# Passage from w_out to the up projection: two operand tiles made beside w_out's last blocks, the embedding's product placed behind w_out, banks and pools laid by order of release

## The chip, the cores and the metric

The kernel runs on one core of a Trainium2 chip. A core has a matrix engine (TensorE, PE in the profile, its weight loads PEld), three engines for elementwise work (VectorE DVE, ScalarE ACT, GpSimd POOL) and a queue engine (SyncE, SP) that here only issues transfers. Each engine runs its own instructions strictly in order and waits where an operand or a buffer of another engine isn't ready. On-chip data lie in SBUF (128 partitions); matmuls write PSUM, whose banks (128x512 fp32 in this program) are handed out by pools too. The metric is the device time of one execution in microseconds (us); less is better.

## What is computed

One decoder layer on x (1 x 1024 x 1024). What matters here is the end of the mixing block, the gated MLP and the per-layer embedding:

```python
h = h + jnp.concatenate([o_a, o_b, o_c], axis=-1) @ w_out[l]
h = h + conv_glu_ffn(rmsnorm(h, norm_ffn_g[l]), ffn_up[l], ffn_conv_w[l], ffn_conv_b[l], ffn_down[l])
gate = jax.nn.sigmoid(rmsnorm(h, norm_ple_g[l]) @ ple_gate[l])
h = h + gate * (p[l] @ ple_proj[l])
...
def conv_glu_ffn(hn, w_up, conv_w, conv_b, w_down):
    u = hn @ w_up                       # 1024 x 5632
    uc = causal depthwise conv of width 3 over u, plus conv_b
    gate, val = jnp.split(uc, 2, axis=-1)
    return (jax.nn.silu(gate) * val) @ w_down
```

`p[l] @ ple_proj[l]` (1024x256 by 256x1024) depends on inputs alone, so it can be computed at any place.

## The kernel before

Activations lie transposed: a tile `h[m]` has 128 of the 1024 features on its partitions and the 1024 positions along its free axis, in two halves of 512. An fp32 product is made of three matmuls on a high and a low part: hi by hi (L127), low of x by hi of w (L129), hi of x by low of w (L131). A high part is a cast on ACT (`whi` L104, operand tiles L1112), a low part a subtraction, for weights of `split_w` on POOL or DVE in turn, by the parity of a counter that also numbers names (L106), for operand tiles on DVE (L1113).

**w_out** (`phase_out`, L1054). Eight blocks of 128 output features. The first pass makes half 0 of all eight blocks, and both halves of blocks 0 and 1; the second pass makes half 1 of blocks 2 to 7. One block of one half is 24 matmuls. Behind a block stand its addition to `h` on DVE (L1073), a store of `h` to DRAM (`hd`, L1074), a square on ACT (L188) and a running sum `acc` on DVE (L189). At the end of each pass `rstd_bcast` makes the norm's factor: four small matmuls sum `acc` over partitions (L159, `ps_ss`), DVE scales (L161), POOL raises to the power -1/2 (L167), four matmuls spread the result over the partitions (L169).

**Operands of the up projection** (`ffn_norm` L1115, `ffn_operands` L1126). `ffn_norm` multiplies `h` by factor and gain (L1122), half 0 first, and splits half 0 into the operand tiles p1 (features 0 to 511) and p2 (the others). The up projection is done in a fast scheme of seven half-size products p1 to p7; p6, p5, p7, p3, p4 need sums of parts of `h` of both halves (L1179, L1181, L1189), and their own splits. `ffn_operands` then issues, for the first two of 22 units: weight loads `raw`, `rav`, the split of the p1 weights, the loads and splits of `pT` and `ple_proj` (L1147, L1148, through the tiles `wraw` of the weights), the products p1 into two G banks, a copy `e` of them to SBUF on ACT (`keep_first`, L1201), the products p2 added onto the same banks, and then the embedding's product: eight blocks of 12 matmuls into V banks, each copied out on ACT (L1167) and stored (L1168) to DRAM for later. After that come p6 to p4 and the loop over units (`phase_up`, L1205): six or seven products of 12 matmuls a unit (L1094), sums of weights on DVE, splits, and behind each unit the convolution, SiLU and gate on ACT and DVE (L1286 to L1295), whose results go to DRAM.

**Down projection** (`phase_down`, L1327). Seven runs over 11 steps k: load `xraw` (L1397), load weights `sr` (L1354), cast and low part of x into `dx` (L1399, L1400), split of the weight, 12 matmuls (L1403). At steps 6 to 9 of the first run `h` is reloaded (L1420).

The order within each engine isn't the order of the code: a scheduler at build time places the instructions, subject to data and to buffers. Which buffer a tile reuses, and so which earlier work it waits for, is set by the pools: a pool that opens takes the room of one that closed, and its first tile waits for the last user of that room.

Of the kernel before, what the change touches and what calls it, by code (L numbers as in the profile page):

```python
# [18 lines left out]
P = 128  # L19
T = 1024  # L20
HT = 512
ND = 8
NFF = 22
EPS = 1e-6
# [4 lines left out]
PC_MIX, PC_FFN, PC_PLE, PC_FIN = 0, 8, 16, 24  # L29
# [50 lines left out]
class Trunk:  # L80
# [57 lines left out]
    def xall(self):  # L138

        X = [({}, {}) for _ in range(ND)]  # L140
        for h in (1, 0):
            for k in range(ND):
                X[k][0][h] = self.xpool.tile([P, HT], F32R, tag=f"xh{k}_{h}", name=self.nm("xh"), bufs=1)
                X[k][1][h] = self.xpool.tile([P, HT], F32R, tag=f"xl{k}_{h}", name=self.nm("xl"), bufs=1)
        return X
# [54 lines left out]
    def build(self):  # L200
        tc, nc = self.tc, self.nc
        with ExitStack() as st:
# [5 lines left out]
            mix, psm = ExitStack(), ExitStack()  # L208
            self.xpool = mix.enter_context(self.pool("x"))
# [7 lines left out]
            up, hs = ExitStack(), ExitStack()  # L217
            self.ep = up.enter_context(self.pool("ep", side="right"))
            hp = hs.enter_context(self.pool("h", side="right"))
# [834 lines left out]
    def phase_out(self, hp, op):  # L1054
# [5 lines left out]
        pbs = []  # L1060
        for hf in (0, 1):
            sl = slice(hf * HT, (hf + 1) * HT)
            acc = op.tile([P, HT], F32, tag="acc", name=self.nm("acc"))
            for m in range(ND):
                t = self.h[m][:, sl]
                if m > 1 or hf == 0:
                    w = self.load_w(self.a["w_out"][m])
                    ps = self.dps.tile([P, T], F32, tag="dp", name=self.nm("dp"))
                    halves = (0, 1) if m < 2 else (hf,)
                    self.dense([ps[:, :HT], ps[:, HT:]], w, self.O, (6, 7, 0, 1, 4, 2, 3, 5), halves)  # L1070
                    for g in halves:
                        u = self.h[m][:, g * HT:(g + 1) * HT]
                        nc.vector.tensor_tensor(u, u, ps[:, g * HT:(g + 1) * HT], ALU.add)  # L1073
                        nc.scalar.dma_start(self.hd[m][g], u)  # L1074
                self.sq_acc(acc, t, m == 0)
            pbs.append(self.rstd_bcast(acc, 1.0 / 1024, EPS, self.mxp))
        return pbs
# [37 lines left out]
    def ffn_norm(self, pbs):  # L1115

        self.TX = {}
        self.op_tiles(self.tpool, "p7", "p6", "p1", "p2", "p5")
        for hf in (0, 1):
            for k in (0, 1, 2, 3, 4, 5, 6, 7) if hf == 0 else (0, 4, 1, 5, 2, 6, 3, 7):  # L1120
                t = self.h[k][:, hf * HT:(hf + 1) * HT]
                self.nc.vector.scalar_tensor_tensor(t, t, self.par[:, PC_FFN + k:PC_FFN + k + 1], pbs[hf],  # L1122
                                                    ALU.mult, ALU.mult)
                if hf == 0:
                    self.op_split("p2" if k >= 4 else "p1", k % 4, t)

    def ffn_operands(self, hs, up):


        nc, h = self.nc, self.h  # L1130
        V, G = nc.vector, nc.gpsimd
        split = self.op_split
        self.units = [{"f": f} for f in range(NFF)]
        first = self.units[:2]
        for d in first:
            d["raw"], d["rav"] = self.load_up(d["f"]), self.load_up(NFF + d["f"])
            d["w1"] = self.split2(d["raw"][:, :HT], V)
        with self.pool("pe") as pp:
            pX, pw = [], []
            for k in (0, 1):  # L1140
                for src, dst, n in ((self.a["pT"][k], pX, "px"), (self.a["ple_proj"][k], pw, "pw")):
                    raw = self.wpool.tile([P, T], F32, tag="wraw", name=self.nm("wraw"), bufs=2)
                    nc.sync.dma_start(raw, src)
                    hi = pp.tile([P, T], F32R, name=self.nm(n + "h"))
                    lo = pp.tile([P, T], F32R, name=self.nm(n + "l"))
                    for c in (slice(0, HT), slice(HT, T)):
                        nc.scalar.copy(hi[:, c], raw[:, c])  # L1147
                        V.tensor_tensor(lo[:, c], raw[:, c], hi[:, c].bitcast(F32), ALU.subtract)  # L1148
                    dst.append((hi, lo))
            self.ped = [self.zpool.tile([P, T], F32, tag=f"pe{m}", name=f"pe{m}") for m in range(ND)]  # L1150
            for d in first:
                d["G"] = self.banks("g")
            self.mul(*[(d["G"][:, :HT], d["w1"], self.TX["p1"], True) for d in first])
            for d in first:
                self.keep_first(d)
            for d in first:
                d["w2"] = self.split2(d["raw"][:, HT:], V)
            self.mul(*[(d["G"][:, :HT], d["w2"], self.TX["p2"], False) for d in first])
            for m in range(ND):
                ps = self.banks("v")  # L1160
                s = slice(m * P, (m + 1) * P)
                for k in (0, 1):
                    (wh, wl), (xh, xl) = pw[k], pX[k]
                    self.mm3({0: ps[:, :HT], 1: ps[:, HT:]}, (wh[:, s], wl[:, s]),
                             ({0: xh[:, :HT], 1: xh[:, HT:]}, {0: xl[:, :HT], 1: xl[:, HT:]}), k == 0, k == 1)
                t = self.wpool.tile([P, T], F32, tag="wraw", name=self.nm("pst"), bufs=2)
                nc.scalar.copy(t, ps)  # L1167
                nc.scalar.dma_start(self.ped[m], t)  # L1168
# [34 lines left out]
    def phase_up(self):  # L1203
        nc, par, ep, cv, TX = self.nc, self.par, self.ep, self.cv, self.TX
        V, G = nc.vector, nc.gpsimd  # L1205
# [24 lines left out]
        def unit(d, prev):  # L1230
# [28 lines left out]
            d["V"] = self.banks("v")  # L1259
# [68 lines left out]
    def phase_down(self, ple):  # L1328
# [14 lines left out]
        for k in (0, 1):  # L1343
            S[k] = xr.tile([P, HT], F32, name=f"sr{k}")
# [212 lines left out]
```

## Time and profile before

| what | value |
|---|---|
| three runs | 1571.83, 1572.70, 1573.13 us (median 1572.7) |
| profiled execution | 1572.51 us, of it the span of the trace 1570.7 us, 1.8 us outside |
| mean granted TensorE clock | 0.974 of full speed |
| w_out's last matmul | issued at 771.98 us of the span |
| first matmul of p6 (the up projection's loop) | 824.97 us |
| first matmul of the down projection | 1233.00 us |

A row of the timeline gives the start in us of the span, the duration, engine, line, operation, result and operand, shape, how many like it follow each other, and in brackets how long the engine stood idle before it and for whom it waited. Matmul durations overlap with each other: what one costs is the distance from start to start. The granted clock is what the chip let TensorE run at in a stretch, 1.00 being full speed.

### The profile page before, as it was taken

Reading aid. Unit: us, or ns where it says so; the run is one execution under the profiler, and the core shown is the slowest. Engines: PE = TensorE matmul, PEld = TensorE weight load, DVE = VectorE, ACT = ScalarE, POOL = GpSimd, SP = SyncE. Lnnn points to the kernel's source line nnn. Section 1 sums busy time; section 2 is a strip of 40 time slices with the busy share of each in tenths; the row PEclk is TensorE's granted clock in tenths of the full one; section 3 lists DMA queues with packets and bytes.
Section 4 is the critical chain, followed back from the end, with each engine's and each line's share of the span. In section 5 each row is a group of like instructions: output and inputs, shape, how many; then the busy total and the mean of one; then the engine's idle time right before and its main releaser. Section 6 shows DMA issues by size and latency. Waiting matters only on the chain.

```text
span 1570.7 us, 20134 instructions
## 1 busy us (share of the span) xinstructions
PE 1490.0 (95%) x7480; PEld 1227.9 (78%) x7480; DVE 1099.8 (70%) x1578; ACT 630.2 (40%) x1079; POOL 429.7 (27%) x353
## 2 busy tenths in 40 slices
PE   7989999989999989999879999999999999999996
PEld 5768998778987777777768888888888778888774
DVE  6378453368547568844768888888888779877584
ACT  6331331322424455523445444444444435455441
POOL 2231411132412123113123455544454000002330
PEclk9989999999999999999999999999999999999998
DMA  5212202123024032054323333333331793351352
GB/s 192 71 58 91 74 28 81 41 74 107 28 84 139 28 108 74 28 202 147 121 110 104 101 101 108 108 101 109 106 113 70 241 327 116 101 167 51 110 173 84
DMA packets 78707, 167.84 MB, mean 107 GB/s; under 512 B 19920, under 2 KB 20048, under 8 KB 78608
## 3 DMA queue, kind: packets, MB, share of 16 engines
q1 hardware_dynamic: 65120, 145.97, 28.6%
q10 hardware_dynamic: 12400, 16.52, 3.1%
q0 software_dynamic: 1088, 4.06, 0.8%
q8 instruction: 59, 0.97, 0.3%
q14 instruction: 40, 0.33, 0.1%
HBM read 120.12 MB, written 46.40 MB: 106 GB/s over the span
## 4 chain that ended last, share of the span: by engine, by line
PE 43%; issue 19%; DVE 5%; POOL 1%; ACT 1%; DMA 1%; POOLq 0%; SPq 0%; DVEq 0%; ACTq 0%
PE bg L1094 15%; PE bv L1094 11%; PE hsc L849 2%; PE swq L993 1%; PE dp L129 1%; PE dp L131 1%; PE dp L127 1%; PE bv L131 1%; PE bv L127 1%; PE swo L1029 1%; PE bv L129 1%; PE swt L1016 1%; PE zp L127 1%; PE zp L129 1%; PE zp L131 1%
## 5 line engine op out<-in xcount | busy, mean ns | idle before, releaser
L127 PE MATMUL dp<-xh,whi 128*128 128x512 f32 x544 | 186.9, 401 | 13.7 <-ACT xh L344 8.6
L131 PE MATMUL dp<-xh,wlo 128*128 128x512 f32 x544 | 185.1, 398 | 1.0 <-POOL wlo L106 1.0
L129 PE MATMUL dp<-xl,whi 128*128 128x512 f32 x544 | 185.3, 398 | 0.7 <-DVE xl L345 0.6
L104 ACT CAST whi<-wraw 128x512 fp32r<-128x512 f32 x120 | 73.4, 619 | 234.5 <-PE dp L129 181.6
L106 POOL TENSOR_TENSOR wlo<-wraw,whi 128x512 fp32r<-128x512 f32 x60 | 83.4, 1390 | 283.6 <-ACT whi L104 242.2
L106 POOL TENSOR_TENSOR wlo<-raw,whi 128x512 fp32r<-128x512 f32 x84 | 134.9, 1624 | 92.7 <-ACT whi L104 92.6
L127 PEld LDWEIGHTS dp<-xh,whi 128*128 128x128 f32 x544 | 103.4, 191 | 36.0 <-ACT xh L344 8.6
L129 PEld LDWEIGHTS dp<-xl,whi 128*128 128x128 f32 x544 | 102.9, 190 | 25.0 <-DVE xl L345 3.0
L131 PEld LDWEIGHTS dp<-xh,wlo 128*128 128x128 f32 x544 | 103.3, 191 | 22.4 <-POOL wlo L106 1.9
L106 POOL TENSOR_TENSOR wlo<-s,whi 128x512 fp32r<-128x512 f32 x44 | 68.0, 1545 | 164.0 <-ACT whi L104 164.0
L1403 PE MATMUL bg<-dx,whi 128*128 128x512 f32 x308 | 96.8, 395 | 2.5 <-DVE dx L1400 2.4
L1403 PE MATMUL bv<-dx,whi 128*128 128x512 f32 x308 | 95.5, 391 | 0.0
L104 ACT CAST whi<-raw 128x512 fp32r<-128x512 f32 x88 | 52.4, 619 | 99.6 <-issue 50.9
L104 ACT CAST whi<-s 128x512 fp32r<-128x512 f32 x66 | 39.0, 619 | 114.8 <-PE bg L1094 112.4
L167 POOL TENSOR_TENSOR rst<-rst,mhalf 128x4 f32<-128x4 f32 x8 | 9.3, 1159 | 257.5 <-DVE rst L161 257.4
L106 DVE TENSOR_TENSOR wlo<-wraw,whi 128x512 fp32r<-128x512 f32 x60 | 50.6, 849 | 41.3 <-ACT whi L104 38.1
L1403 PEld LDWEIGHTS bg<-dx,whi 128*128 128x128 f32 x308 | 57.3, 189 | 17.7 <-ACT whi L104 3.5
L1403 PEld LDWEIGHTS bv<-dx,whi 128*128 128x128 f32 x308 | 58.1, 189 | 12.3
L1399 ACT CAST dx<-xraw 128x512 fp32r<-128x512 f32 x77 | 47.9, 622 | 49.1 <-PE bv L1403 28.1
L1400 DVE TENSOR_TENSOR dx<-xraw,dx 128x512 fp32r<-128x512 f32 x77 | 54.8, 712 | 4.8 <-ACT dx L1399 4.6
L286 DVE TENSOR_TENSOR dp<-dp,rstd 128x512 f32<-128x512 f32 (+1 forms) x26 | 23.2, 898 | 46.6 <-PE dp L131 44.7
L1403 PE MATMUL bg<-dx,wlo 128*128 128x512 f32 x154 | 48.0, 393 | 1.1 <-DVE wlo L106 1.1
(403 smaller groups left out, 3871.8 us busy)
## 6 DMA issues: line engine op xcount, KB each, us to landing
raw<-in_ffn_up_dram SPq DMA_DIRECT2D x44, 512.0 KB, 3.7
wraw<-in_w_in_dram SPq DMA_DIRECT2D x30, 512.0 KB, 3.7
z<-zst SPq DMA_DIRECT2D x18, 512.0 KB, 3.2
gb<-ct SPq DMA_DIRECT2D x33, 256.0 KB, 2.3
xraw<-gb SPq DMA_DIRECT2D x33, 256.0 KB, 2.8
xraw<-gt SPq DMA_DIRECT2D x33, 256.0 KB, 2.7
zl<-z SPq DMA_DIRECT2D x16, 512.0 KB, 4.3
wraw<-in_ple_gate_dram SPq DMA_DIRECT2D x16, 512.0 KB, 3.7
```

The source lines that it names most:

```text
L104: nc.scalar.copy(hi, src)
L106: eng.tensor_tensor(lo, src, hi.bitcast(F32), ALU.subtract)
L127: nc.tensor.matmul(ps[hf], wh, xh[hf], start=first, stop=False)
L129: nc.tensor.matmul(ps[hf], wh, xl[hf], start=False, stop=False)
L131: nc.tensor.matmul(ps[hf], wl, xh[hf], start=False, stop=last)
L286: self.nc.vector.tensor_tensor(ps, ps, r, ALU.mult)
L849: nc.tensor.matmul(sc[:, c, :], ks[:, c * P:(c + 1) * P], view(qt, c * P, [2 * n, 64 // n], [HT + n, 2], [1, n]), start=True, stop=True)
L993: nc.tensor.matmul(pq[h][:, b:b + w], d["q"][hs, qb * P:nk], d["k"][hs, b:b + w], start=True, stop=True)
L1094: nc.tensor.matmul(ps, w[part == 2][:, s], X[k][part == 1], start=start and k == part == 0, stop=k == 3 and part == 2, skip_group_check=no ...
L1399: nc.scalar.copy(xh, x)
L1400: V.tensor_tensor(xl, x, xh.bitcast(F32), ALU.subtract)
L1403: nc.tensor.matmul(ps[m], wt[part == 2][:, m * P:(m + 1) * P], (xh, xl)[part == 1], start=k == part == 0, stop=k == NK - 1 and part == 2)
```

## The change

The two passes of w_out and what follows are put together in another way. Half 0 is finished first, then block 2 of half 1, and then the factor of half 0. Blocks 3 to 7 of half 1 follow, and between them, two steps to a block, half 0 is normed and split into p1 and p2; `pT` and `ple_proj` are loaded and split there too, through tiles of their own. The factor of half 1 is made at the end, the first units' weights are loaded and split, and the embedding's product follows w_out directly, into the banks (`dps`) that w_out used. Then come the norm of half 1, p1, the copies `e`, p2, and the other operands.

To make room, the split x tiles lie in one pool for each half; half 0's closes early. p1 and p2 have a pool of their own. The V banks are claimed before the G banks. In the down projection the tiles `xraw`, `dx` and two of the weights `sr` lie on the right side, in the place of others, and the remaining `sr` and the reloaded `h` on the left.

```diff
-                X[k][0][h] = self.xpool.tile([P, HT], F32R, tag=f"xh{k}_{h}", name=self.nm("xh"), bufs=1)
+                X[k][0][h] = self.xpool[h].tile([P, HT], F32R, tag=f"xh{k}", name=self.nm("xh"), bufs=1)
...
-            pbs = self.phase_out(hp, mix.enter_context(self.pool("acc")))
-            mix.close()
+            with self.pool("px", side="right") as self.pxp:
+                pb = self.phase_out(hp, mix[0])
+            mix[1].close()
+            self.ffn_norm(1, pb)
+            psm.close()
             self.tpool = up.enter_context(self.pool("tx"))
-            self.ffn_norm(pbs)
-            psm.close()
+            self.op_tiles(self.tpool, "p6", "p5", "p7")
...
+        for m in range(ND):
+            rows(m, (0, 1) if m < 2 else (0,))
+            self.sq_acc(acc, self.h[m][:, :HT], m == 0)
+        rows(2, (1,))
+        pb = self.rstd_bcast(acc, 1.0 / 1024, EPS, self.mxp)
+        x0.close()
+        self.TX = {}
+        self.op_tiles(self.tp12, "p1", "p2")
+        self.ped = [self.zpool.tile([P, T], F32, tag=f"pe{m}", name=f"pe{m}") for m in range(ND)]
+        with self.pool("pw") as pwp:
+            px, pw = [], []
+            parts = [(px, self.pxp, "pT", 0), (pw, pwp, "ple_proj", 0), (px, self.pxp, "pT", 1), (pw, pwp, "ple_proj", 1)]
+            norm = self.ffn_norm(0, pb)
+            for m in range(3, ND):
+                rows(m, (1,))
+                for _ in range(2):
+                    next(norm, None)
+                if parts:
+                    self.pe_load(pwp, *parts.pop(0))
             for m in range(ND):
...
+                self.sq_acc(acc, self.h[m][:, HT:], m == 0)
+            pb = self.rstd_bcast(acc, 1.0 / 1024, EPS, self.mxp)
+            self.ffn_first()
+            for m in range(ND):
+                ps = self.dps.tile([P, T], F32, tag="dp", name=self.nm("dp"))
+                s = slice(m * P, (m + 1) * P)
+                for k in (0, 1):
+                    (wh, wl), (xh, xl) = pw[k], px[k]
+                    self.mm3({0: ps[:, :HT], 1: ps[:, HT:]}, (wh[:, s], wl[:, s]),
+                             ({0: xh[:, :HT], 1: xh[:, HT:]}, {0: xl[:, :HT], 1: xl[:, HT:]}), k == 0, k == 1)
+                t = self.wpool.tile([P, T], F32, tag="wraw", name=self.nm("pst"), bufs=2)
+                nc.scalar.copy(t, ps)
+                nc.scalar.dma_start(self.ped[m], t)
+        return pb
+
+    def pe_load(self, raws, dst, pool, src, k):
+        raw = raws.tile([P, T], F32, tag="praw", name=self.nm("praw"), bufs=2)
+        self.nc.sync.dma_start(raw, self.a[src][k])
+        hi, lo = (pool.tile([P, T], F32R, name=self.nm(n)) for n in ("peh", "pel"))
+        for c in (slice(0, HT), slice(HT, T)):
+            self.nc.scalar.copy(hi[:, c], raw[:, c])
+            self.nc.vector.tensor_tensor(lo[:, c], raw[:, c], hi[:, c].bitcast(F32), ALU.subtract)
+        dst.append((hi, lo))
...
         for d in first:
...
+            d["V"] = self.banks("v")
+        for d in first:
+            d["G"] = self.banks("g")
+        self.mul(*[(d["G"][:, :HT], d["w1"], self.TX["p1"], True) for d in first])
+        for d in first:
+            self.keep_first(d)
+        for d in first:
+            d["w2"] = self.split2(d["raw"][:, HT:], V)
+        self.mul(*[(d["G"][:, :HT], d["w2"], self.TX["p2"], False) for d in first])
...
-        hp = ple.enter_context(self.pool("h2", side="right"))
+        xr = ple.enter_context(self.pool("xr", side="right"))
+        xb = [xr.tile([P, HT], F32R, name=f"dx{i}") for i in range(8)]
+        xs = [xr.tile([P, HT], F32, name=f"xraw{i}") for i in range(6)]
+        S = {k: xr.tile([P, HT], F32, name=f"sr{k}") for k in (0, 1)}
         wst = self.wst = ple.enter_context(self.pool("ws", side="right"))
         wa = aa.enter_context(self.pool("wa", side="right"))
-        xr = ple.enter_context(self.pool("xr"))
-        S = {}
-        for k in (6, 7, 8, 9, 10, 2, 3, 4, 5):
-            S[k] = xr.tile([P, HT], F32, name=f"sr{k}")
-        xb = [xr.tile([P, HT], F32R, name=f"dx{i}") for i in range(8)]
-        xs = [xr.tile([P, HT], F32, name=f"xraw{i}") for i in range(6)]
-        for k in (0, 1):
-            S[k] = xr.tile([P, HT], F32, name=f"sr{k}")
+        xl = ple.enter_context(self.pool("xl"))
+        for k in range(2, NK):
+            S[k] = xl.tile([P, HT], F32, name=f"sr{k}")
+        hp = ple.enter_context(self.pool("h2"))
```

What the scheduler makes of it stands in the instruction orders. Each row has the line, the operation, and result and operands by their numbered names. The first place is PE at the end of w_out, before: behind the last matmul of w_out (`dp`) stand the sum of squares of half 1, the spread of its factor and the first matmuls of p1.

```order
L127 MATMUL dp_6065<-xh_5367,whi_6061 128x512
L129 MATMUL dp_6065<-xl_5368,whi_6061 128x512
L131 MATMUL dp_6065<-xh_5367,wlo_6063 128x512
L159 MATMUL ps_ss_6095<-few,acc_5850 128x1 x4
L169 MATMUL ps_ss_6096<-cst,rst_1233_6103 128x128 x4
L1094 MATMUL bg_6250<-tp1h_6130,whi_6195 128x512
L1094 MATMUL bg_6251<-tp1h_6130,whi_6203 128x512
```

The same place after the change (`peh` and `pel` are the embedding's operands, `dp` its banks):

```order
L131 MATMUL dp_6135<-xh_5370,wlo_6133 128x512
L127 MATMUL dp_6214<-peh_5966,peh_6017 128x512 x2
L129 MATMUL dp_6214<-pel_5967,peh_6017 128x512 x2
L131 MATMUL dp_6214<-peh_5966,pel_6018 128x512 x2
L127 MATMUL dp_6214<-peh_6068,peh_6119 128x512 x2
L129 MATMUL dp_6214<-pel_6069,peh_6119 128x512 x2
L131 MATMUL dp_6214<-peh_6068,pel_6120 128x512 x2
L127 MATMUL dp_6230<-peh_5966,peh_6017 128x512 x2
L159 MATMUL ps_ss_6184<-few,acc 128x1 x4
L129 MATMUL dp_6230<-pel_5967,peh_6017 128x512 x2
L169 MATMUL ps_ss_6185<-cst,rst_1243_6192 128x128 x4
L131 MATMUL dp_6230<-peh_5966,pel_6018 128x512 x2
```

Between the last matmul of w_out and the sum of squares now stand 14 matmuls of the embedding, and two more ahead of the spread; p1 comes after all 96 of them.

The second place is ACT ahead of the copies `e` of p1, before (`tp5h`, `tp6h` are operand tiles of p5 and p6, `nu` a sum of parts of `h`):

```order
L1112 CAST tp5h_6146<-h_5433 128x512
L1112 CAST tp5h_6148<-h_5434 128x512
L1112 CAST tp6h_6122<-nu_6442 128x512
L1112 CAST tp6h_6124<-nu_6447 128x512
L1112 CAST tp5h_6150<-h_5435 128x512
L1112 CAST tp6h_6126<-nu_6453 128x512
L1112 CAST tp5h_6152<-h_5436 128x512
L104 CAST whi_6618<-s_1282_6605 128x512
L1201 COPY e_6276<-bg_6250 128x512
```

And after (`pst` is the copy of an embedding block on its way to DRAM):

```order
L1109 COPY pst_6339<-dp_6326 128x1024
L1155 CAST tp6h_6358<-nu_6450 128x512
L1110 DMA pe_5917<-pst_6339 128x1024
L1155 CAST tp6h_6360<-nu_6455 128x512
L1155 CAST tp6h_6362<-nu_6461 128x512
L1155 CAST tp5h_6366<-h_5439 128x512
L1155 CAST tp5h_6368<-h_5440 128x512
L1155 CAST tp5h_6370<-h_5441 128x512
L1155 CAST tp6h_6364<-nu_6467 128x512
L1155 CAST tp5h_6372<-h_5442 128x512
L1225 COPY e_6413<-bg_6387 128x512
```

The eight casts still stand ahead of the copies, now behind the last embedding block.

The third place is the passage to the down projection. ACT before (`ct` is the convolution's result, first of unit 20 and then of unit 21, `dx` the cast x and `whi` from `sr` the cast weight of the down projection):

```order
L1290 ACTIVATE ct_9691<-ct_9691 128x1024
L1286 ACTIVATE ct_9724<-bv_9540,par,ncw 128x1024
L1399 CAST dx_9852<-xraw_9860 128x512
L1286 ACTIVATE ct_9791<-bg_9663,par 128x1024
L104 CAST whi_9910<-sr_9866 128x512
L1399 CAST dx_9854<-xraw_9861 128x512
L104 CAST whi_9930<-sr_9867 128x512
```

ACT after:

```order
L1315 ACTIVATE ct_9697<-ct_9697 128x1024
L1311 ACTIVATE ct_9730<-bv_9546,par,ncw 128x1024
L1311 ACTIVATE ct_9797<-bg_9669,par 128x1024
L1311 ACTIVATE ct_9815<-bv_9702,par,ncw 128x1024
L1315 ACTIVATE ct_9797<-ct_9797 128x1024
L1423 CAST dx_9841<-xraw_9849 128x512
L104 CAST whi_9920<-sr_9855 128x512
```

The first cast of x now stands behind all three activations of the last unit. SP's queue there, before (`gb` and `gt` are gated results stored to DRAM):

```order
L1298 DMA gb_6534<-ct_9691 128x512
L1312 DMA gt_6600<-t_1846_9816 128x512
L1397 DMA xraw_9860<-gb_6524 128x512
L1354 DMA sr_9866<-in_ffn_down_dram 128x512
L1397 DMA xraw_9861<-gb_6525 128x512
```

SP after:

```order
L1323 DMA gb_6542<-ct_9697 128x512
L1337 DMA gt_6608<-t_1844_9822 128x512
L1378 DMA sr_9866<-in_ffn_down_dram 128x512
L1378 DMA sr_9867<-in_ffn_down_dram 128x512
...
L1378 DMA sr_9872<-in_ffn_down_dram 128x512
L1444 DMA h_0_0_9878<-hd_0_5447 128x512
L1421 DMA xraw_9849<-gb_6532 128x512
```

Seven loads of weights and one of `h` now go ahead of the first load of x.

More of the change, by code (lines that the diff above doesn't have):

```diff
@@ L1059, in phase_out @@
             nc.scalar.dma_start(self.h[k], self.a["xT"][k])
[L1060 to L1063, printed above, removed]
-            for m in range(ND):
[L1065 to L1076, printed above, removed]
@@ L1077, in phase_out, with rows @@
-        return pbs
+        acc = hp.tile([P, HT], F32, name="acc")
+        def rows(m, halves):
+            w = self.load_w(self.a["w_out"][m])
+            ps = self.dps.tile([P, T], F32, tag="dp", name=self.nm("dp"))
+            self.dense([ps[:, :HT], ps[:, HT:]], w, self.O, (6, 7, 0, 1, 4, 2, 3, 5), halves)
+            for g in halves:
+                u = self.h[m][:, g * HT:(g + 1) * HT]
+                nc.vector.tensor_tensor(u, u, ps[:, g * HT:(g + 1) * HT], ALU.add)
+                nc.scalar.dma_start(self.hd[m][g], u)
@@ L1113, in op_split, with ffn_norm, steps, ffn_first @@
         self.nc.vector.tensor_tensor(lo, src, hi.bitcast(F32), ALU.subtract)
[L1115 to L1119, printed above, removed]
+    def ffn_norm(self, hf, pb):
+        def steps():
             for k in (0, 1, 2, 3, 4, 5, 6, 7) if hf == 0 else (0, 4, 1, 5, 2, 6, 3, 7):
                 t = self.h[k][:, hf * HT:(hf + 1) * HT]
-                self.nc.vector.scalar_tensor_tensor(t, t, self.par[:, PC_FFN + k:PC_FFN + k + 1], pbs[hf],
-                                                    ALU.mult, ALU.mult)
+                self.nc.vector.scalar_tensor_tensor(t, t, self.par[:, PC_FFN + k:PC_FFN + k + 1], pb, ALU.mult, ALU.mult)
                 if hf == 0:
                     self.op_split("p2" if k >= 4 else "p1", k % 4, t)
+                yield
+        return steps() if hf == 0 else list(steps())
+    def ffn_first(self):
+        self.units = [{"f": f} for f in range(NFF)]
+        for d in self.units[:2]:
+            d["raw"], d["rav"] = self.load_up(d["f"]), self.load_up(NFF + d["f"])
+        for d in self.units[:2]:
+            d["w1"] = self.split2(d["raw"][:, :HT], self.nc.vector)
     def ffn_operands(self, hs, up):
@@ L1132, in ffn_operands @@
         split = self.op_split
-        self.units = [{"f": f} for f in range(NFF)]
         first = self.units[:2]
         for d in first:
[L1136 to L1139, printed above, removed]
-            for k in (0, 1):
[L1141 to L1168, printed above, removed]
```

16 lines of the change are left out of this document (10 added, 6 removed).

## The prediction

> **What bounds the kernel now.** I began with the page's busy shares and the chain that ended last.
>
> ```profile
> PE 1490.0 (95%) x7480; PEld 1227.9 (78%) x7480; DVE 1099.8 (70%) x1578; ACT 630.2 (40%) x1079; POOL 429.7 (27%) x353
> PE 43%; issue 19%; DVE 5%; POOL 1%; ACT 1%; DMA 1%; POOLq 0%; SPq 0%; DVEq 0%; ACTq 0%
> ```
>
> TensorE is busy 95% of the span and carries the chain. So an edit pays only where PE stands still or runs slowly. The windows around the passage come next (columns: stretch, length, busy us and instructions of PE, PEld, DVE, ACT, POOL, then granted clock, DMA share, GB/s).
>
> ```profile
> 770.00:780.00 10.00, 4.14 (x20) 3.35 (x19) 7.15 (x12) 7.48 (x14) 4.02 (x3) 0.84 0.32 106
> 780.00:790.00 10.00, 8.64 (x32) 6.75 (x31) 10.00 (x17) 1.00 (x2) 0.00 (x0) 0.82 0.00 0
> 790.00:800.00 10.00, 3.36 (x8) 2.68 (x9) 10.00 (x18) 5.74 (x11) 1.81 (x1) 0.70 0.00 0
> ```
>
> In these 30 us PE is busy 16, at clocks of 0.84, 0.82 and 0.70, while DVE is full for 20 of them: here the elementwise work is the bound. PE's waits between 700 and 840 us name the places (total us, times, longest):
>
> ```profile
> PE bg L1094 <- ACT e L1201: 8.0, 1, 8.0
> PE ps_ss L159 <- DVE acc L189: 4.1, 1, 4.1
> PE ps_ss L169 <- POOL rst L167: 2.5, 2, 1.7
> PE dp L127 <- ACT whi L104: 2.3, 1, 2.3
> PE dp L131 <- POOL wlo L106: 0.7, 1, 0.7
> ```
>
> The PE timeline of the passage puts them in order.
>
> ```profile
> 771.98 0.39 PE L131 MATMUL dp<-xh,wlo 128*128 128x512 f32 x1
> 776.51 1.52 PE L159 MATMUL ps_ss<-few,acc 128*128 128x1 f32 x8 [4.14 <-DVE acc L189]
> 779.75 1.11 PE L169 MATMUL ps_ss<-cst,rst 128*128 128x128 f32 x4 [1.72 <-POOL rst L167]
> 780.51 1.20 PE L1094 MATMUL bg<-tp1h,whi 128*128 128x512 f32 x2
> 788.02 0.61 PE L129 MATMUL bv<-pxl,pwh 128*128 128x512 f32 x2
> 796.64 0.79 PE L1094 MATMUL bg<-tp2h,whi 128*128 128x512 f32 x1 [8.01 <-ACT e L1201]
> 804.12 0.61 PE L131 MATMUL bv<-pxh,pwl 128*128 128x512 f32 x2
> 824.97 0.39 PE L1094 MATMUL bv<-tp6h,whi 128*128 128x512 f32 x1
> ```
>
> w_out ends at 771.98 + 0.39 = 772.37. The first p6 matmul stands at 824.97. That is 52.6 us for 24 matmuls of p1, 96 of the embedding and 24 of p2. From 804.12 to 824.97 there are 92, so one takes 0.2267 us and 144 take 32.65. The other 20 us are three waits (4.14 + 1.72 + 8.01 = 13.9), the norm's small matmuls (1.52 + 1.11 = 2.6) and, for the rest, slow matmuls, 3.5 us: p1 begins with 1.20 for a pair where 0.61 is usual.
>
> **Part 1: the factor of half 0.** Before, two w_out matmuls stand between sum and spread, and PE still waits 0.76:
>
> ```profile
> 740.37 0.95 PE L159 MATMUL ps_ss<-few,acc 128*128 128x1 f32 x8
> 742.66 0.65 PE L169 MATMUL ps_ss<-cst,rst 128*128 128x128 f32 x4 [0.76 <-POOL rst L167]
> ```
>
> Now six stand there, 4 x 0.2267 = 0.9 us more cover; but the sum is queued directly behind block 2's matmuls, so DVE has that block's addition to do ahead of the scaling (one operation, 0.68 by the row of L189 below). About 0.76 - 0.9 + 0.6 = 0.46 remains: **-0.3** (0 to -0.76).
>
> **Part 2: the first pass of w_out.** At block 3's first weights PE has this:
>
> ```profile
> 707.47 0.50 PE L127 MATMUL dp<-xh,whi 128*128 128x512 f32 x1 [2.32 <-ACT whi L104]
> 708.87 0.79 PE L131 MATMUL dp<-xh,wlo 128*128 128x512 f32 x1 [0.67 <-POOL wlo L106]
> 712.02 0.40 PE L127 MATMUL dp<-xh,whi 128*128 128x512 f32 x1
> ```
>
> The counter's parity has moved, so the low half waited for at 708.87 is now made on DVE, which by the rows below takes 0.6 to 0.7 us where POOL takes 1.26: **-0.5** (0 to -0.67). The 2.32 stays. From 707.47 to 712.02 there are nine matmuls in 4.55 us; without 9 x 0.2267 = 2.04 and the wait of 0.67, 1.8 us are left for slow matmuls. So a gap of 2.3 us costs some 2 us more behind it, a price used below. With both parts w_out ends at about 771.6.
>
> **Part 3: norm and splits beside w_out's blocks 3 to 7.** In DVE's new order 39 operations stand from the first factor (L161) to the addition of block 7, p1's and p2's eight low parts and the embedding's among them.
>
> ```profile
> 774.02 1.75 DVE L1227 TENSOR_TENSOR s<-s,raw 128x512 f32<-128x512 f32 x1 [0.56 <-POOL wlo L106]
> 775.69 0.68 DVE L189 TENSOR_TENSOR acc<-acc,sqt 128x512 f32<-128x512 f32 x1
> 778.15 2.49 DVE L1113 TENSOR_TENSOR tp1l<-h,tp1h 128x512 fp32r<-128x512 f32 x4
> 773.95 1.26 POOL L106 TENSOR_TENSOR wlo<-raw,whi 128x512 fp32r<-128x512 f32 x1
> ```
>
> Four in 2.49 make 0.62 each, so 39 x 0.62 = 24.2 us, in five blocks of 24 x 0.2267 = 5.44, or 27.2 us. An operation that meets POOL takes 1.75 instead of 0.68, so 1.07 more; four POOL low parts stand there, up to 4.3 us: 28.5 at most. DVE is nearly full, but PE needs only the weights from it. The low part of block 6 is behind 18 of these operations and block 4's addition, so ready about 13 us into the stretch and needed at 16.3; that of block 7 at about 17.7, needed at 21.8. Slack of 3.3 and 4 us: **0** (if DVE fell behind by more than that, rival 1).
>
> [...]
>
> **Part 4: the passage.** Its new order: 14 embedding matmuls (3.2 us), the sum of squares (0.95 and 0.65 for the spread, by part 1's rows), two more matmuls, the spread, 80 embedding matmuls, p1, four matmuls of p6, p2. The waits that remain: `acc` needs, after block 7's addition, a square on ACT and a sum on DVE; before it waited 4.14, with 3.2 now covering it and up to 1.3 us of DVE lag: 0.5 taken (0 to 1.9). POOL's factor: 1.72 less two matmuls 0.45 and a DVE that is not in the middle of other work: 1.0 taken (0.5 to 1.3). The embedding then lies over the norm of half 1 and the sums for p6 that kept DVE full from 780 to 800, so those are ready when p1 ends.
>
> Then the 8.01 us wait. It is not the copy itself:
>
> ```profile
> 789.00 1.16 ACT L1112 CAST tp5h<-h 128x512 fp32r<-128x512 f32 x2 [10.36 <-DVE h L1179]
> 796.01 1.07 ACT L1201 COPY e<-bg 128x512 f32<-128x512 f32 x2
> 825.17 1.01 ACT L1167 COPY pst<-bv 128x1024 f32<-128x1024 f32 x1 [1.71 <-PE bv L131]
> ```
>
> p1 was done before 788.02, but ACT is in order, and eight casts stood ahead of the copies, waiting for DVE's sums of `h`. After the change the casts still stand ahead, but the last embedding copy (1.01) is the only thing ahead of them that follows PE. The eight casts at 0.55 take 4.4 us; p1 lasts 5.4. Copies at p1's end, 1.07, less the four p6 matmuls that PE has meanwhile (0.9), and a cast or two late: 0.9 taken (0.2; up to 8 if DVE's sums are late, rival 2).
>
> Sum: 32.65 + 0.95 + 0.65 + 0.5 + 1.0 + 0.9 = 36.65, taken as 36.8, with no gap over 1.1 us and so no slow stretch: the 3.5 us of slow matmuls go too (behind part 5's gap of 1.08 a pair took 0.74, behind its 2.44 it took 0.97). 36.8 - 52.6 = **-15.8**. What PE waited for, 13.9 us, now lies under the embedding's matmuls; without that cover it would come back in full.
>
> **Part 5: the passage to the down projection.** Buffers moved, and this place gets worse.
>
> ```profile
> 1233.00 0.71 PE L1403 MATMUL bg<-dx,whi 128*128 128x512 f32 x2
> 1236.18 0.74 PE L1403 MATMUL bg<-dx,wlo 128*128 128x512 f32 x2 [1.08 <-DVE wlo L106]
> 1240.76 0.97 PE L1403 MATMUL bg<-dx,whi 128*128 128x512 f32 x2 [2.44 <-DVE dx L1400]
> 1244.09 0.81 PE L1403 MATMUL bg<-dx,whi 128*128 128x512 f32 x2
> 1231.22 1.21 ACT L1286 ACTIVATE ct<-bg,par 128x1024 f32<-128x1024 f32 x1 [0.45 <-DVE bg L1321]
> 1237.41 1.06 ACT L1290 ACTIVATE ct<-ct 128x1024 f32<-128x1024 f32 x1
> 1227.45 0.38 SPq L1397 DMA_DIRECT2D xraw<-gb  x1
> 1227.92 0.41 SPq L1354 DMA_DIRECT2D sr<-in_ffn_down_dram  x1
> xraw<-gb SPq DMA_DIRECT2D x11, 256.0 KB, 5.5
> ```
>
> Before, steps 0 and 1 take from 1233.00 to 1244.09: 24 matmuls (5.44 us), waits of 1.08 and 2.44, a slow stretch after the latter. Now ACT makes both convolutions and the SiLU ahead of the first cast: the second needs PE's end at 1233.2 and a DVE addition, so 1233.9 + 1.2 + 1.06 + two casts of 0.6 = 1237.4. And SP issues eight loads ahead of `xraw`: at 0.47 apart the issue comes at 1231.2, or at about 1232.9 if it waits until an earlier load has landed (5.5 us by the last row). So x lands between 1236.7 and 1238.4. I take the later one, since the transfers are queued by then: PE starts at 1238.2 after a gap of 5 us, pays 2 us of slow matmuls, and has the following operands at hand: 1238.2 + 5.44 + 2 = 1245.6, taken 1245.4, **+1.3**; and +0.4 for step 9, whose loads now stand behind the reloads of `h`. **+1.7** (-3.5 if x comes at once and nothing else waits; +7 if the eight loads push it back by a landing more).
>
> The up and down loops have the same instructions in the same order; the scheduler's rows differ in names only.
>
> **Sum:** -0.3 - 0.5 + 0 - 15.8 + 1.7 = -14.9, from 1572.51 to 1557.6. The profiled run lies 0.19 under the median, so **1557.8 us**.
>
> **Rivals.** (1) *DVE starves w_out.* Norm, splits and sums fill DVE to 24 to 29 of 27 us. If the weights' low parts come late at each of blocks 3 to 7, each pays a gap as at 707.47: 2.3 + 0.7 + 2.2 slow, 5.2 us, five times 26. Net 1557.8 + 26 = 1584, slower. It decides from the point where DVE lags over 3.3 us; against it stand the counts of part 3. [...] 0.05. (2) *The wait for `e` stays.* The eight casts wait for DVE's sums, which begin only after the second factor; p1 ends 25 us after w_out, and 8 norms, 8 sums and p6's and p5's low parts, some 24 operations of 0.65, need 16 of the 18.1 us of the 80 matmuls. If they don't fit, up to 8 us come back: 1566. 0.12. (3) *Late operands inside the up projection.* adding up DVE's and POOL's new order at the durations above, I find p7's weight of the first unit only some 0.7 us ahead of its use; PE arrives 15 us earlier at a DVE that has as much to do: +3 to 5, 1562. 0.15. (4) *The down passage gains.* With x at hand early, -3.5 instead of +1.7: about 1553. 0.08. That the change does not do what it says is ruled out by the order: the embedding does stand ahead of the sum.
>
> **Chances.** The forecast has 0.60, within 1555 to 1561. 0.2% of the time, 3.1 us, is about what these runs tell from no change. Faster by more: all but rival 1 and mixed mishaps, 0.92; within 0.02; slower 0.06. The range goes down to rival 4 with parts 1 and 2 at their bounds, 1552, and up to rival 2, 1566.
>
> **What would show it.** Right: in the profile after, no PE wait over 1.5 us from w_out's end to p6, this stretch near 37 us, clock 1.00; the wait for `e` about 1; PE's gap ahead of L1423 some 5 us. Wrong: PE waiting for `wlo` or `whi` inside w_out, windows of DVE at 10.00 there, or a p2 that waits 3 us and more.

## The result and the profile after

The changed kernel takes 1572.25 us, the median of 12 runs, the kernel before 1571.87 us in 12 runs beside them; the ratio is 1.0004, 95% interval 0.9989 to 1.0018. 1557.8 was forecast: the change was to win 14.9 us and wins nothing that can be measured.

Yet the passage went as worked out. PE's waits of the changed kernel between 690 and 840 us (total us, times, longest):

```profile
PE dp L127 <- ACT whi L104: 2.3, 1, 2.3
PE bv L1137 <- DVE v L1290: 1.2, 1, 1.2
PE ps_ss L169 <- POOL rst L167: 1.1, 2, 0.8
PE bg L1137 <- ACT e L1225: 0.7, 1, 0.7
PE ps_ss L159 <- DVE acc L189: 0.4, 1, 0.4
```

The waits of 8.0, 4.1 and 1.7 us are down to 0.7, 0.4 and 0.8. The PE timeline of the changed kernel from the end of w_out on:

```profile
761.78 0.39 PE L131 MATMUL dp<-xh,wlo 128*128 128x512 f32 x1
762.00 0.63 PE L127 MATMUL dp<-peh,peh 128*128 128x512 f32 x2
763.41 0.63 PE L127 MATMUL dp<-peh,peh 128*128 128x512 f32 x2
765.84 1.02 PE L159 MATMUL ps_ss<-few,acc 128*128 128x1 f32 x8 [0.40 <-DVE acc L189]
768.20 0.65 PE L169 MATMUL ps_ss<-cst,rst 128*128 128x128 f32 x4 [0.77 <-POOL rst L167]
787.43 0.63 PE L1137 MATMUL bg<-tp1h,whi 128*128 128x512 f32 x2
794.86 0.50 PE L1137 MATMUL bg<-tp2h,whi 128*128 128x512 f32 x1 [0.72 <-ACT e L1225]
```

The embedding starts where w_out ends and covers the norm. But look at the distances: from 762.00 to 763.41 are six matmuls of the embedding, 0.235 us each, with a granted clock of 1.00. Before, they stood 0.2267 apart. This goes on for the rest of the program. Two long stretches in which PE never stands still, one of the up projection and one of the down projection (columns: stretch, length, busy us and instructions of PE, PEld, DVE, ACT, POOL, then granted clock, DMA share, GB/s; the number behind PE's busy time counts its matmuls). Before:

```profile
900.00:1100.00 200.00, 200.00 (x884) 165.60 (x883) 177.81 (x180) 81.27 (x114) 99.48 (x63) 1.00 0.33 106
1310.00:1400.00 90.00, 90.00 (x399) 74.53 (x398) 77.00 (x126) 45.43 (x76) 0.00 (x0) 1.00 0.45 131
```

After:

```profile
900.00:1100.00 200.00, 200.00 (x866) 162.58 (x865) 175.65 (x175) 79.76 (x111) 99.29 (x63) 1.00 0.31 100
1310.00:1400.00 90.00, 90.00 (x385) 72.34 (x385) 70.44 (x114) 43.25 (x72) 0.00 (x0) 1.00 0.42 123
```

In the same time, at the same granted clock and with PE busy throughout, it does 866 matmuls instead of 884, and 385 instead of 399. Busy share and waits can't show this; the counts do. The groups by line say which matmuls are slow (changed kernel, 840 to 1200 us; count, then busy us and mean duration of one in ns, which overlaps with the next one's):

```profile
L1137 PE MATMUL bg<-tp3h,whi 128*128 128x512 f32 x76 | 30.6, 402 | 0.5 <-DVE x L1300 0.5
L1137 PE MATMUL bg<-tp1h,whi 128*128 128x512 f32 x76 | 30.0, 395 | 0.0
L1137 PE MATMUL bv<-tp4h,whi 128*128 128x512 f32 x73 | 28.4, 389 | 0.0
L1137 PE MATMUL bv<-tp6h,whi 128*128 128x512 f32 x73 | 28.4, 389 | 0.0
```

All four took 389 before. p6 and p4 still do. p1, whose tiles have moved to the right side, and p3, whose matmuls stand between p1's, don't. So it isn't the clock of the whole engine.

The span by stretches, from the PE timeline of the profiled executions (us; the four p6 matmuls done early, 0.9 us, are counted in the up projection; the last column is the experiment e5 of the next section):

| stretch | before | after | forecast of the difference | measured | e5 |
|---|---|---|---|---|---|
| w_out, first matmul to last | 117.7 | 115.3 | -0.8 | -2.4 | 115.4 |
| passage, to the end of p2 and embedding | 52.6 | 37.5 | -15.8 | -15.1 | 36.8 |
| rest of the up projection | 408.2 | 418.7 | 0 | +10.5 | 411.1 |
| to step 2 of the down projection | 10.9 | 12.7 | +1.3 | +1.7 | 13.4 |
| rest of the down projection | 208.4 | 212.6 | +0.4 | +4.2 | 205.8 |
| to the end | 118.2 | 119.7 | 0 | +1.5 | 118.2 |
| sum | 916.1 | 916.6 | -14.9 | +0.5 | 900.7 |

The changed kernel's profiled execution took 1565.21 us, the shortest of its twelve; its span is 1563.4. It is shorter than the profiled one of before by 7 us, mostly because of a stretch that the change doesn't touch: in the mixing phase, ahead of w_out, PE waits twice for ACT's `bb`, 9.8 us in all before and 3.1 in the changed kernel; e5, too, has 9.8. That is why stretches are compared here. They come from one execution of each kernel, though. In e3 and e11 below, which have the instruction order of the kernel before, the stretch to step 2 took 8.6 us where the table has 10.9, and the last stretch took 117.5 us in e2 where the table has 118.2.

### The profile page after: what moved, and what is told of

Its sections match the earlier page's. It is cut to its first block, busy times and chain, and to the rows that moved or that the text cites. A ratio compares the mean times of both kernels' runs of the same rounds, so it can differ in the third digit from the quotient of the medians.

```text
span 1563.4 us, 20128 instructions
## 1 busy us (share of the span) xinstructions
PE 1494.6 (96%) x7480; PEld 1218.9 (78%) x7480; DVE 1096.4 (70%) x1578; ACT 629.2 (40%) x1079; POOL 428.7 (27%) x353
## 4 chain that ended last, share of the span: by engine, by line
PE 56%; DVE 5%; issue 4%; POOL 2%; DMA 1%; ACT 1%; SPq 0%; POOLq 0%; ACTq 0%; DVEq 0%
PE bg L1137 14%; PE bv L1137 10%; PE bg L1427 7%; PE bv L1427 7%; PE dp L131 2%; PE dp L129 2%; PE dp L127 2%; PE hsc L854 2%; PE swq L998 1%; POOL wlo L106 1%; PE swo L1034 1%; PE swt L1021 1%; PE zp L127 1%; PE zp L129 1%; PE bg L127 1%
## 5 line engine op out<-in xcount | busy, mean ns | idle before, releaser
L104 ACT CAST whi<-s 128x512 fp32r<-128x512 f32 x66 | 38.8, 619 | 127.2 <-PE bg L1137 118.3
```

The lines of the kernel that those rows point to most:

```text
L104: nc.scalar.copy(hi, src)
```

## The experiments

What the slow matmuls have in common was read from the built programs: where their operand tiles start in a partition, modulo 512 bytes (all differences between tiles of one side are multiples of 512).

```
                                  before   after
weights (whi, wlo; embedding's)    320      320
moving tiles of the left side      320      320   (x of w_out; p6 p5 p7 p3 p4; dx before)
moving tiles of the right side     480      480   (before: 192 matmuls of the gate projection;
                                                   after: embedding, p1, p2, dx too, 1740 in all)
```

In both kernels matmuls of 512 columns whose moving tiles are at 480 follow each other every 0.234 us in the mean, and those at 320 every 0.227, the gate projection's halves among them: right side 0.234, left side 0.227, with the same weights. (Where the two kinds alternate, as p1 and p3 do, both are slowed: 395 and 402 ns in the groups above, against 389.) Three theories: the right side is slow (B); a start 32 off a multiple of 64 is slow (A); or TensorE got slower because it rests less (C).

**e1 to e4: shifts of 32 and 64 bytes.** No instruction differs in any of them, only addresses.

```diff
 e1, on the changed kernel (e2: the same on the kernel before)
             self.zpool = e(tc.tile_pool(name="z", bufs=1, space=bass.MemoryType.DRAM))
+            e(self.pool("pad", side="right")).tile([P, 8], F32, name="pad")
 e3, on the kernel before
-        few = cp.tile([P, 8], F32, name="few")
+        few = cp.tile([P, 16], F32, name="few")
 e4, on the changed kernel
+            e(self.pool("pad", side="right")).tile([P, 16], F32, name="pad")
             self.ep = up.enter_context(self.pool("ep", side="right"))
```

> The changed kernel with 32 bytes per partition reserved at the top of SBUF, so that every tile on the right side starts 32 bytes lower, at a multiple of 64; no instruction differs. Theory A (a matmul whose moving tile starts 32 bytes off a multiple of 64 is slower): the embedding, p1/p2 with their partners and the down projection go back to 0.227 us from start to start, means of 389 ns; 9 + 0.7 + 7 + 1.4 us less, about 17 us under the changed kernel, 1555 us, ratio to before about 0.99. Theory B (the right side, the high addresses themselves, are slow): no difference, 1572. Theory C (the finer clock sinks because TensorE rests less): no difference, 1572.

> The kernel before with the same 32 bytes reserved; only the gate projection at the end reads moving tiles on the right side there (192 matmuls). Theory A: 192 x 7.5 ns, 1.4 us less than before. Theories B and C: no difference.

> The kernel before with a constant tile made 32 bytes larger, so that every tile on the left side starts 32 bytes off a multiple of 64; the order of the instructions is unchanged. Theory A: all 5116 matmuls of 512 columns are now off, 4924 more than before, up to 4924 x 7.5 ns = 37 us slower, less what falls into waits: 1595 to 1610 us. Theories B and C: no difference, 1572.

> The changed kernel with 64 bytes reserved at the top in place of 32, so that all right side tiles move but stay 32 bytes off a multiple of 64. Theory A: as the changed kernel, 1572 us, the slow groups at 395 to 401 ns. A theory by which any shift of the tiles helps: about 1555.

Measured, each against the kernel before on the same chip: e1 1565.68 us, ratio 0.996 (0.9943 to 0.9976); e2 1571.19 us, 0.9999 (0.9987 to 1.001); e3 1569.02 us, 0.9977 (0.9961 to 0.9993); e4 1567.66 us, 0.9975 (0.9961 to 0.9988). The two stretches of e1, e3 and e4, in this order:

```profile
900.00:1100.00 200.00, 200.00 (x877) 164.07 (x876) 175.82 (x179) 82.52 (x114) 96.97 (x62) 1.00 0.31 101
1310.00:1400.00 90.00, 90.00 (x389) 72.96 (x389) 74.12 (x121) 44.70 (x74) 0.00 (x0) 1.00 0.44 127
```

```profile
900.00:1100.00 200.00, 200.00 (x885) 165.60 (x884) 177.62 (x180) 81.25 (x114) 99.38 (x63) 1.00 0.32 106
1310.00:1400.00 90.00, 90.00 (x399) 74.53 (x398) 76.63 (x126) 45.17 (x76) 0.00 (x0) 1.00 0.46 132
```

```profile
900.00:1100.00 200.00, 200.00 (x871) 163.19 (x870) 175.18 (x177) 82.48 (x114) 96.86 (x62) 1.00 0.30 100
1310.00:1400.00 90.00, 90.00 (x387) 72.43 (x386) 74.80 (x122) 44.75 (x74) 0.00 (x0) 1.00 0.42 126
```

Theory A falls twice: in e3 all matmuls are 32 off a multiple of 64 and none is slower (399 matmuls in the second stretch, as before), and in e1 none is off and dx stays slow (389 matmuls there). C falls with e1 and e4 against the changed kernel: the same instructions in the same order, other counts (877 and 871 in the first stretch, where the changed kernel has 866). e2 brings its 192 matmuls from 0.234 to 0.233 us and no time that shows. e3's ratio lies a little under 1; nothing here explains that, and it is not the sign that A asks for. What e3 left alone is the distance between moving tile and weights (the difference of their starts), since both moved by 32. That makes a fourth theory, D: a matmul is slow where the two start at different places. F is its rival: the places 320 and 352 are fast by themselves.

**e5 and e6: the distance.** e5 moves the right side by 160 bytes, so that its tiles start at 320 as well. e6, on the kernel before, moves all left side tiles but the weights by 32.

```diff
 e5, on the changed kernel (e11: the same on the kernel before)
+            e(self.pool("pad", side="right")).tile([P, 40], F32, name="pad")
             self.ep = up.enter_context(self.pool("ep", side="right"))
 e6, on the kernel before (the pool of the weights, "w", is opened ahead of this place)
             self.zpool = e(tc.tile_pool(name="z", bufs=1, space=bass.MemoryType.DRAM))
+            e(self.pool("pad")).tile([P, 8], F32, name="pad")
```

> The changed kernel with 160 bytes reserved at the top of the right side, so that its moving tiles start at 320 modulo 512, as the weights and all left side tiles do; no instruction differs. Theory D (a matmul is slower where moving tile and weight tile start at different places modulo 512) and theory F (320 and 352 are fast places by themselves, 416 to 480 slow ones): every group at 389 ns and 0.227 us apart, 9 + 0.7 + 7 + 1.4 us less than the changed kernel, about 1555 us, ratio 0.989. Theory B (the right side is slow wherever its tiles start): as the changed kernel or as e1, 1566 to 1572.

> The kernel before with 32 bytes put between the pool of the weights and all other left side tiles: weights stay at 320 modulo 512, moving tiles go to 352, the place at which they were fast in e3, where the weights stood at 352 too. Theory D: some 4900 matmuls lose 5 to 7 ns, 25 to 35 us slower, 1597 to 1607. Theory F: no change, 1572. Theory B: no change, 1572.

e5 took 1556.59 us, ratio 0.9904 (0.9886 to 0.9922). e6 took 1598.16 us, ratio 1.0171 (1.015 to 1.0192). e5's stretches, then e6's:

```profile
900.00:1100.00 200.00, 200.00 (x884) 165.62 (x883) 176.51 (x179) 83.55 (x116) 100.77 (x65) 1.00 0.31 103
1310.00:1400.00 90.00, 90.00 (x399) 74.53 (x398) 70.67 (x115) 44.54 (x73) 0.00 (x0) 1.00 0.43 126
```

```profile
900.00:1100.00 200.00, 200.00 (x858) 160.65 (x858) 175.34 (x175) 80.78 (x113) 96.06 (x61) 1.00 0.31 100
1310.00:1400.00 90.00, 90.00 (x387) 72.04 (x386) 78.08 (x128) 41.87 (x70) 0.00 (x0) 1.00 0.40 123
```

With 160 bytes the changed kernel is 14.9 us faster than the one before, with the right side still in use (B falls), and 32 bytes between weights and moving tiles cost the kernel before 27 us (1598.16 against 1571.47 beside it). In e3 and e6 the moving tiles start at the same place, 352; only the weights differ, 352 there and 320 here (F falls). e6 holds its own control. The embedding's weights lie behind the added bytes, at 352 like its moving tiles; the weights of the up projection don't. The end of the one and the begin of the other in e6's PE timeline:

```profile
831.25 0.61 PE L129 MATMUL bv<-pxl,pwh 128*128 128x512 f32 x2
831.70 0.62 PE L131 MATMUL bv<-pxh,pwl 128*128 128x512 f32 x2
832.16 0.39 PE L1095 MATMUL bv<-tp6h,whi 128*128 128x512 f32 x1
...
834.96 0.39 PE L1095 MATMUL bg<-tp5h,whi 128*128 128x512 f32 x1
```

From 831.25 to 832.16 are four matmuls: 0.227 us for one. From 832.16 to 834.96 are twelve, in 2.80 us: 0.233. The step from one to the other comes with the first matmul whose distance isn't zero.

**e8: the period.** The room allows 64 for the embedding, p1 and p2, and 256 for dx (with five tiles `xraw` in place of six).

```diff
+            e(self.pool("pad", side="right")).tile([P, 24], F32, name="pad")
             self.ep = up.enter_context(self.pool("ep", side="right"))
...
+        ple.enter_context(self.pool("pad2", side="right")).tile([P, 80], F32, name="pad2")
         xr = ple.enter_context(self.pool("xr", side="right"))
...
-        xs = [xr.tile([P, HT], F32, name=f"xraw{i}") for i in range(6)]
+        xs = [xr.tile([P, HT], F32, name=f"xraw{i}") for i in range(5)]
...
-                x = xs[self.ix % 6]
+                x = xs[self.ix % 5]
```

> The changed kernel with other distances from the weights' place: embedding, p1 and p2 64 bytes off, dx and the gate projection's right half 256 off (for the room, five tiles xraw in place of six). Theory D with a period of 512: both kinds slow, 395 to 402 ns by group. With a period of 256: dx back at 389 ns, p1 and p2 slow. With a period of 64: all at 389; this is hardly open, since 128 was slow in e1.

One run, 1556.5 us; its mixing phase was short, as in the changed kernel's profile, so the time says little and the counts are read:

```profile
900.00:1100.00 200.00, 200.00 (x870) 163.03 (x869) 176.36 (x176) 79.96 (x112) 99.71 (x63) 1.00 0.31 101
1310.00:1400.00 90.00, 90.00 (x399) 74.55 (x398) 70.57 (x114) 44.47 (x74) 0.00 (x0) 1.00 0.43 127
```

At 256 dx is as fast as at 0 (399 matmuls), at 64 p1 and p2 are slow (870 in the first stretch). So 256 counts as 0, and I take the distance modulo 256; 192 and 224 were not tried. From start to start, the mean over matmuls that follow one of the same distance, of all these kernels: 0 and 256, 0.227 us; 64, 0.229 (the embedding alone); 128, 0.232; 32, 0.233; 96, 0.233; 160, 0.234. In the up projection, where p1 and p2 alternate with matmuls at distance 0, the order is another: the counts of the first stretch are 866 at 160, 870 at 64, 871 at 96, 877 at 128 and 884 at 0. How much a distance costs thus hangs on the neighbours too.

**e7 and e9: the down projection's tiles.** e9 puts them back where the kernel before has them and leaves the rest of the change. e7 is e5 with dx, xraw and all weights `sr` on the left, in this order, and h, ws, wa on the right.

```diff
 e7, with the line of e5
+        hp = ple.enter_context(self.pool("h2", side="right"))
         wst = self.wst = ple.enter_context(self.pool("ws", side="right"))
         wa = aa.enter_context(self.pool("wa", side="right"))
+        xr = ple.enter_context(self.pool("xr"))
+        xb = [xr.tile([P, HT], F32R, name=f"dx{i}") for i in range(8)]
+        xs = [xr.tile([P, HT], F32, name=f"xraw{i}") for i in range(6)]
+        S = {k: xr.tile([P, HT], F32, name=f"sr{k}") for k in range(NK)}
```

> e5 with the down projection's first tiles (dx, xraw, all sr) on the left side, in the place of p6, p5, p7, which are free early, and h, ws, wa on the right as in the kernel before. Theories D and F: as e5, and the gap ahead of the down projection shrinks from 5.2 to some 3 us, 2 us less than e5: 1553. If the first load of x is not what ends the gap: as e5.

> The changed kernel with the down projection's tiles where the kernel before has them, nothing reserved. Theories B, D and F alike: dx at 389 ns again, 7 us less than the changed kernel, and 2 us from the gap: 1563, ratio 0.994; the up projection stays slow (395 to 401 ns).

e9 took 1566.92 us, ratio 0.9967 (0.9955 to 0.9979), where 1563 was expected: dx's matmuls are fast again and p1 to p3 stay slow (398 matmuls in the second stretch, 866 in the first). But the stretch of the later steps comes down by 2.3 us only, from 212.6 to 210.3, since with the old places PE waits three more times for the weights' `whi`, 2.4 us together, and starts slowly behind some waits (from 1260 to 1400 us `bg<-dx,whi`, which waits 1.0 us for `whi`, took 392 ns in the mean, the other groups 389). And the gap ahead of the down projection shrinks by less than 1 us. ACT's rows there, then PE's:

```profile
1228.29 1.20 ACT L1311 ACTIVATE ct<-bv,par,ncw 128x1024 f32<-128x1024 f32 x1 [2.02 <-DVE bv L1349]
1229.40 0.61 ACT L1424 CAST dx<-xraw 128x512 fp32r<-128x512 f32 x1
1231.52 1.22 PE L1428 MATMUL bg<-dx,whi 128*128 128x512 f32 x2 [4.50 <-ACT whi L104]
```

It is 4.50 us where the changed kernel has 5.25, though the tiles lie as in the kernel before: ACT still makes both convolutions of the last unit ahead of the first cast of x, and by these rows that order, not the place of the tiles, makes most of the gap.

e7 took 1554.68 us, ratio 0.9897 (0.9877 to 0.9918), not to be told from e5. Its gap ahead of the down projection is 4.5 us where e5 has 5.4 and 3 was expected, but the later steps, 205.8 us in e5, take 208.4, as in the kernel before: the new places do help the rest of the down projection by 2.6 us, once their distance is right.

**e11: how much of e5 is the change's own.**

> The kernel before with the 160 bytes of e5 reserved. Theory D: only the gate projection's 192 matmuls on the right side gain, 192 x 7 ns = 1.3 us, ratio 0.999; so against e5 nearly all of the 15 us are the change's own.

1569.63 us, ratio 0.9988 (0.9974 to 1.0002): the 160 bytes alone bring the kernel before what its 192 matmuls promise, or nothing (its last stretch, with these matmuls, takes 118.2 us as before). e5 and e7 beat both kernels, and nearly all of it is the change.

## Why the prediction was wrong

**The step that failed** is the sentence "The up and down loops have the same instructions in the same order; the scheduler's rows differ in names only." It is true of the instructions, but it put the moved tiles at zero. They cost what the passage gained: by the stretches of e5 against those of the changed kernel, 0.7 us in the passage (the embedding itself), 7.6 in the rest of the up projection and 6.8 in the down projection, 15.1 together. None of the four rivals has such a cost, and the kernel's standing still, which came, had been given only 0.02. (The 1.5 us of the last stretch are not the distance's: its 192 matmuls were at 480 before as well, and e9, with the same places, took 118.3 there.) The diff says "pool" and "side" and the order shows the waits that follow from it; neither shows an address, and I weighed places only by when they come free. By e6 against e3 a distance of 32 bytes cost 29 us (1598.16 and 1569.02). Why a distance costs time, and why one of 256 bytes doesn't (399 matmuls in e8's second stretch, as at 0), no run here shows.

**Parts 1 and 2** (-0.8): -2.4. The wait for the factor is 0.4 us where 0.46 was left over, and the low half isn't waited for any more. The other 1.6 us are mostly slow matmuls behind the gap of 2.32 us, which did not come in this execution. In e1 and e4, which have the same order, they came, with more at another place, and w_out took 118.4 and 118.3 us; so this gain is luck of the execution in good part (more below).

**Part 3** (0): right. Up to w_out's end PE waits only for the 2.3 us that it had before and for the 0.4; DVE did not starve w_out, so rival 1 is out. Nor does every operation that meets POOL take 1.75 us: in the changed kernel, beside POOL's low parts, an addition to `h` at 740.44 took 0.69 and a low part of the embedding at 746.49 took 1.70.

**Part 4** (-15.8): -15.1 with the slow embedding, -15.8 in e5. The three waits were taken at 0.5, 1.0 and 0.9 and came to 0.40, 0.77 and 0.72; rival 2 is out.

**Part 5** (+1.7): +1.7 to step 2, where +1.3 was worked out. The gap is as priced, the difference is in part luck: from 1240 to 1246 us the kernel before had a granted clock of 0.72 in its profile, and behind the same place e11 had 1.00 and a wait of 1.48 in place of 2.44. Against e11's 8.6 us the changed kernel's 12.7 are 4.1 more. ACT's rows in the changed kernel, then SP's and PE's:

```profile
1219.72 1.20 ACT L1311 ACTIVATE ct<-bv,par,ncw 128x1024 f32<-128x1024 f32 x1 [2.02 <-DVE bv L1349]
1220.90 1.06 ACT L1315 ACTIVATE ct<-ct 128x1024 f32<-128x1024 f32 x1
1222.35 0.62 ACT L1423 CAST dx<-xraw 128x512 fp32r<-128x512 f32 x1 [0.39 <-DMA xraw<-gb]
```

```profile
1212.50 3.29 SPq L1378 DMA_DIRECT2D sr<-in_ffn_down_dram  x7
1216.14 0.33 SPq L1444 DMA_DIRECT2D h<-hd  x1
1216.58 0.36 SPq L1421 DMA_DIRECT2D xraw<-gb  x1
```

```profile
1223.70 1.22 PE L1427 MATMUL bg<-dx,whi 128*128 128x512 f32 x2 [5.25 <-ACT whi L104]
```

Both chains that were priced end together: the second convolution and SiLU are through at 1221.96, and x, issued behind eight other loads, is there at 1222.35. "Buffers moved" was the reason given for this place; e9 shows that the places make less than 1 us of the gap. The +0.4 for step 9 was wrong in sign; with the right distance the later steps gain 2.6.

**Rival 3** (late operands in the up projection, +3 to 5) is there in small. In e5, where no distance slows the matmuls, the rest of the up projection takes 2.9 us more than before. PE waits ahead of p7 of the first two units (0.18 and 1.20 us) and of p3 of the third (0.71), where before it waited nowhere in this stretch. The longest:

```profile
827.79 0.47 PE L1138 MATMUL bv<-tp7h,whi 128*128 128x512 f32 x1 [1.20 <-DVE v L1291]
```

That row names DVE's `v`, an addition that still reads the bank, as what came last, not p7's weights, which the prediction had counted as late. With +2.9 of rival 3 and the gains of w_out and of the down projection, e5's -15.4 lands on the forecast of -14.9 by terms that offset each other.

## What to carry to other kernels

When an edit moves tiles, compare where the moving operand and the weights of each matmul start, modulo 256 bytes: a difference cost 1 to 4% of the matmul's time here (0.229 to 0.235 us from start to start against 0.227; 256 was tried in e8 alone), and 160 bytes reserved at one end repaired it (e5, 1556.59 us against 1571.47 beside it). To find such a loss, count matmuls per window at a granted clock of 1.00, or take the distance from start to start; busy share and waits look better than before while it happens (PE 96% in the changed kernel, 95% before). And a stretch that gained what was forecast, in a kernel that gained nothing, is a reason to compare the stretches that were thought unchanged.

## What the runs showed of the hardware that was not expected

The distance of 32 to 160 bytes between moving tile and weights costs 2 to 7 ns per matmul of 512 columns (0.229 to 0.234 us against 0.227), and it can slow matmuls at distance 0 beside them. In the changed kernel (160) p3 took 402 ns between p1's 395; in e1 (128) it stayed at 388 to 390. In e4 (96) and e8 (64) it reaches further: p7, which follows the block of p2 and p5 at distance 0, stands 0.230 us apart in the mean, where e1 and e5 have 0.227. Why is open.

The same gap of 2.32 us in w_out is followed by slow matmuls at a lower granted clock in some executions and not in others. Changed kernel, then e1, which differs by addresses alone, each with the window of 3 us behind the gap:

```profile
699.67 0.50 PE L127 MATMUL dp<-xh,whi 128*128 128x512 f32 x1 [2.32 <-ACT whi L104]
...
702.66 0.39 PE L131 MATMUL dp<-xh,wlo 128*128 128x512 f32 x1
699.67:702.67 3.00, 2.91 (x12) 2.10 (x13) 1.37 (x3) 0.99 (x2) 1.45 (x1) 1.00 0.39 92
```

```profile
708.46 0.50 PE L127 MATMUL dp<-xh,whi 128*128 128x512 f32 x1 [2.32 <-ACT whi L104]
...
712.98 0.40 PE L131 MATMUL dp<-xh,wlo 128*128 128x512 f32 x1
708.46:711.46 3.00, 2.91 (x7) 2.09 (x8) 1.36 (x3) 0.98 (x2) 1.44 (x1) 0.62 0.38 94
```

Twelve matmuls each: 2.99 us from first to last at a granted clock of 1.00 in the one, 4.52 in the other, with 0.62 over the first 3 us. Of the kernels with the changed order, e1 and e4 were slow there (4.5 us), and the changed kernel, e5, e7, e8 and e9 fast (3.0). All with the order of the kernel before were slow (4.8 to 5.2 us, a second wait of 0.67 among them). One execution of each has a trace, so what decides isn't shown; a price taken from one such gap holds to within 1.5 us only.
